# A weight stream of a two-layer trunk on one core: blocks split one by one, or in pairs

## The chip, the cores and the metric

The kernel runs on one core of one Trainium2 chip. The metric is the device time of the program in microseconds (us), one launch, inputs in HBM. TensorE multiplies, VectorE, ScalarE and GpSimd work beside it on tiles of 128 partitions in the on-chip memory, and SyncE issues the loads. The profile calls them PE, DVE, ACT, POOL and SP.

## The reference, cut to what matters

Two layers on 256 tokens of width 1024. Layer 0 mixes by latent attention, layer 1 by attention whose keys an indexer selects; a PEER expert mixer stands behind each. Everything is float32.

```python
for i in range(2):
    m = mla(x) if i == 0 else dsa(x)            # 8 heads; x @ w_in, ..., o @ w_o
    x = layernorm(ALPHA * x + m)
    f = peer(x)
    x = layernorm(ALPHA * x + f)

def peer(x):                                    # 16384 experts = 128 x 128 keys
    q = x @ w_q                                 # 8 heads x 2 halves
    v1, i1 = top_k(q1 @ keys1, 16); v2, i2 = top_k(q2 @ keys2, 16)
    best, pos = top_k(v1[:, None] + v2[None, :], 16)
    gate = softmax(best); expert = i1 * 128 + i2 at pos
    return sum_e gelu(x . w_down[e]) * gate[e] * w_up[e]
```

## The kernel before

**Weights.** All large weights come as 604 blocks of 128 x 1024 floats, in the order of their use, through one `Stream`, `ws`. A block is loaded by SyncE's queue into a tile `raw` (L73), rounded by ScalarE into `hi` (the cast, L85), and `lo = raw - hi` is made by VectorE, in places by GpSimd (the subtraction, L89). Tokens are split likewise into `xh` and `xl`. A product is three matmuls: hi by xh, hi by xl, lo by xh (all matmuls have line L198).

**Buffers and lead.** `raw`, `hi` and `lo` have four buffers of one block each. `get()` hands out block i, has the blocks up to i + 3 split (`AHEAD`) and those up to i + 6 loaded (`DMA_AHEAD`), as buffers come free: a cast into a `hi` tile waits until TensorE has read the block that was there four earlier.

**Stages.** The order in which the program gives work to an engine is kept by each engine; a scheduler moves some of it at build time. The stages of the trace, in order:

- latent attention (to 101 us): input blocks, 7 blocks of `mla_qk`, 2 of values, 8 of the out projection (tiles `y`);
- PEER of layer 0: 16 blocks of queries (tiles `pq`), then 128 blocks of `w_down` (tiles `d`, `proj`, 24 matmuls a block), then 128 of `w_up` (tiles `y`, `rows`, 12 matmuls of 512 columns a block);
- sparse attention of layer 1 (from about 935 us): values 8 blocks, indexer queries 4 and one narrow block of keys (`dsa_ik`), 16 of queries and keys, 8 of the out projection. There `share = 3` gives every third block's subtraction to GpSimd;
- PEER of layer 1, as that of layer 0.

Beside the `d` blocks VectorE and GpSimd pick the experts. `choose()` is a generator of small steps, of which each block takes one or two, from about 165 to 300 us (and 1135 to 1270 us). In its tail each step is a compare of 128 x 800 (L635, VectorE), a multiplication (L637, GpSimd) and a reduction (L640, VectorE). Then `prepare` and `place`, four tokens at a time, make one-hot rows (L681 GpSimd, L682 VectorE, L683 ScalarE) and multiply them on TensorE into tiles `G` (to about 500 us, and again in layer 1). In the `w_up` stage each second block has a cast and a subtraction of 128 x 512 for its tokens (L737, L738).

**Finish.** `finish()` takes the last four blocks of a row product (`STAGGER`) without splitting further ones ahead, does token tile 0 on all four, then tile 1, so that the layer norm of tile 0 (L252 to L261; Square on ScalarE, L255; a power on GpSimd, L258) lies beside the matmuls of tile 1. Then it sets `to_pool = TO_POOL`: the next two subtractions go to GpSimd.

Of the kernel before, what the change touches and what calls it, by code (L numbers as in the profile page):

```python
# [10 lines left out]
F32 = mybir.dt.float32  # L11
F32R = mybir.dt.float32r
# [3 lines left out]
ALU = mybir.AluOpType  # L16
AX = mybir.AxisListType

P = 128
T = 256  # L20
D = 1024
# [19 lines left out]
CELLS = sum(SEG)  # L41
STAGGER = 4
STEPS = (2, 1)
TO_POOL = 2
GSCALE = 2.0 ** 14
TINY = 2.0 ** -40
DSA_POOL = 3
# [1 line left out]


class Stream:
    """Weight blocks [128, w] in order of use, each split into two float32r parts."""

    AHEAD = 3
    DMA_AHEAD = 3

    def __init__(self, tc, nc, raw, hi, lo):
        self.tc, self.hold = tc, None
        self.nc, self.raw, self.hi, self.lo = nc, raw, hi, lo
        self.blocks, self.ready = [], []  # L60
        self.n_loaded = self.n_split = self.n_taken = 0
        self.tiles = []
        self.to_pool = 0
        self.share = 0

    def add(self, src, w=D):
        self.blocks += [(src[i], w) for i in range(src.shape[0])]

    def _load(self, upto):
        while self.n_loaded <= min(upto, len(self.blocks) - 1):  # L70
            src, w = self.blocks[self.n_loaded]
            t = self.raw.tile([P, D], F32, tag="raw", name=f"raw{self.n_loaded}")
            self.last = self.nc.sync.dma_start(t[:, :w], src).ins  # L73
            self.tiles.append(t)
            self.n_loaded += 1

    def _split(self, upto):
        nc = self.nc
        while self.n_split <= min(upto, len(self.blocks) - 1):
            w = self.blocks[self.n_split][1]  # L80
            self._load(self.n_split)
            raw = self.tiles[self.n_split][:, :w]
            hi = self.hi.tile([P, D], F32R, tag="hi", name=f"hi{self.n_split}")[:, :w]
            lo = self.lo.tile([P, D], F32R, tag="lo", name=f"lo{self.n_split}")[:, :w]
            nc.scalar.copy(hi, raw)  # L85
            eng = nc.gpsimd if self.to_pool > 0 or (self.share and self.n_split % self.share == 0) else nc.vector
            self.to_pool -= 1
            with self.tc.issue_after(self.hold) if self.hold is not None else nullcontext():
                eng.tensor_tensor(lo, raw, hi.bitcast(F32), op=ALU.subtract)  # L89
            if eng is nc.vector:  # L90
                self.hold = None
            self.ready.append((hi, lo))
            self.n_split += 1

    def get(self, ahead=None):
        i = self.n_taken
        self.n_taken += 1
        self.fill(i + (self.AHEAD if ahead is None else ahead))
        return self.ready[i]

    def fill(self, upto):
        self._split(upto)
        self._load(upto + self.DMA_AHEAD)


class Arena:
# [27 lines left out]
def tile_trunk(ctx: ExitStack, tc: tile.TileContext, ins, out: bass.AP):  # L134
    nc = tc.nc
    def pool(name, bufs, **kw):
        return ctx.enter_context(tc.tile_pool(name=name, bufs=bufs, **kw))
# [3 lines left out]
    big = pool("big", 1)  # L141
    small = pool("small", 3)
    ohp = pool("ohp", 2)
    raws = pool("raws", 4)
    his = pool("his", 4)
    los = pool("los", 4)
    psp = pool("psp", 4, space=bass.MemoryType.PSUM)
    pyp = pool("pyp", 1, space=bass.MemoryType.PSUM)

# [30 lines left out]
    ws = Stream(tc, nc, raws, his, los)  # L180
# [23 lines left out]
        mm(o, ll, rh, False, stop)  # L204

    def proj(o, blk, w=P):
        """o[w, 256] = block^T x^T over all of D."""
        h, l = blk
        for c in range(NC):
            s = slice(c * w, (c + 1) * w)  # L210
            mm3(o, (h[:, s], l[:, s]), (xh[:, c, :], xl[:, c, :]), c == 0, c == NC - 1)
# [21 lines left out]
        return ins  # L233

    def rows(o4, lhs, blk, start, stop, tiles=(0, 1)):
        """o4[t][nh] += lhs(t)^T block, for a moving block [128, 1024]."""
        h, l = blk
        lh, ll = lhs
        for t in tiles:
            tsl = slice(t * P, (t + 1) * P)  # L240
            todo = [(w, rr, i, n) for i, (w, rr) in enumerate(((lh, h), (lh, l), (ll, h))) for n in range(2)]
            if stop:
                todo.sort(key=lambda z: z[3])
            for w, rr, i, n in todo:
                ins = mm(o4[t][n], w[:, tsl], rr[:, n * 512 : (n + 1) * 512], start and i == 0, stop and i == 2)
        return ins
# [15 lines left out]
        return mean.ins  # L262

    def finish(y4, lhs_of, n, g, b, x, spare, after):
        """The last blocks of a row product, token tile by token tile, each with its layer norm."""
        blks = [ws.get(ahead=0) for _ in range(STAGGER)]
        last = None
        for t in range(2):
            with ExitStack() as order:
                if last is not None:  # L270
                    order.enter_context(tc.issue_after(last.ins))
                for i, blk in enumerate(blks):
                    k = n - STAGGER + i
                    last = rows(y4, lhs_of(k), blk, k == 0, k == n - 1, (t,))
            mean = layernorm(x[t], y4[t], g, b, spare[t], spare[2 + t], spare[4])
        for t in range(2):
            with tc.issue_after(mean):
                done = after(t, spare[t])
        ws.to_pool = TO_POOL
        ws.hold = done.ins if done is not None else None  # L280
# [18 lines left out]
        nc.vector.tensor_tensor(o, t1, xs, op=ALU.add)  # L299

    def attention(qk, v, mask, scale, oh, ol, ar, meanwhile):
        """qk(h) lists (qT, kT) pairs whose products add up; o^T in two parts."""
        sring = ar.ring(6, T)
        tring = ar.ring(2, 384)
        probs = {}
# [57 lines left out]
    def mla():  # L363
        ar = Arena(arena, 0, 30720)
        cos, sin = load_rope(ar, "c_rope64")
        norm = ar.take(5)
# [18 lines left out]
                    nc.gpsimd.tensor_tensor(sq[:, lo, :], sq[:, lo, :], sq[:, i, :], op=ALU.add)  # L385

        def inverse_rms(lo, hi, k):
            """[128 tokens, 2]: one over the root mean square of each token's latent."""
            p = ps(f"ms{k}")
            for t in range(2):  # L390
                mm(p[:, t : t + 1], sq[:, lo, t * P : (t + 1) * P], ones, True, True)
            nc.vector.tensor_scalar(rms[:, k, :], p[:, 0:2], 1.0 / (P * (hi - lo)), RMS_EPS, op0=ALU.mult, op1=ALU.add)
            nc.gpsimd.tensor_tensor(rms[:, k, :], rms[:, k, :], mhalf.to_broadcast([P, 2]), op=ALU.pow)
            return rms[:, k, :]
# [8 lines left out]
        parts = []  # L403
        for i in range(3):
            nc.vector.tensor_scalar(nrm[:, i, :], where[i], norm[:, i : i + 1], None, op0=ALU.mult)
            h, l = [z[i // 2].rearrange("p a b -> p (a b)")[:, (i % 2) * T : (i % 2) * T + T] for z in gq]
# [161 lines left out]
    def peer(li):  # L568
        last = li == DEPTH - 1
# [114 lines left out]
                onehot[g4].append((V, U, L))  # L684

        def place(g4, done):
            """Scatter the gates of four tokens; blocks under `done` already hold gelu."""
            p = py(g4 % 4, f"G{g4}")
            for j, (V, U, L) in enumerate(onehot.pop(g4)):
                mm(p[:, j * P : (j + 1) * P], V, U, True, False)  # L690
# [150 lines left out]
```

## Time and profile before

| what | value |
|---|---|
| time, median of three runs | 1910.81 us (1908.92 to 1911.19) |
| profiled execution, span | 1908.3 us |
| TensorE busy | 97% of the span, granted clock 0.9 or more in 39 of 40 slices |
| VectorE busy | 71%, from five to nine tenths and more by slice |
| ScalarE busy | 55% |
| GpSimd busy | 30%, near full only where one-hot rows are made |
| DMA engines busy | 53% of 16 engines, 332.87 MB |

The span is the time from the first to the last instruction of one profiled execution on the core. No time other than its span is shown for that execution; the three runs lie 0.6 to 2.9 us above it, and the median 2.5 us. Busy shares are means over stages that have different limits.

### The profile page before, as it was taken

The numbers are of one execution on the slowest core, as the hardware profiler recorded it, in microseconds if no ns is written. First come the engines' busy times: TensorE is split into PE (matmuls) and PEld (weight loads), VectorE is DVE, ScalarE is ACT, GpSimd is POOL, SyncE is SP. The second block draws the span as 40 slices with busy tenths as digits, with TensorE's granted clock in tenths as the row PEclk, the third lists the DMA queues.
The fourth block names the chain that finished last, engine by engine and source line by source line (L and its number), as shares of the span: only waits on it lengthen the run. The fifth ranks groups of instructions, "written<-read, shape, count | busy, mean of one in ns | idle before, by whom it ended". The sixth has DMA issues, their size and how long they took to land.

```text
span 1908.3 us, 33460 instructions
## 1 busy us (share of the span) xinstructions
PE 1858.4 (97%) x12562; PEld 1677.8 (88%) x12562; DVE 1359.1 (71%) x2765; ACT 1057.2 (55%) x1833; POOL 580.1 (30%) x654
## 2 busy tenths in 40 slices
PE   8989999999999999999998899999999999999998
PEld 7789999999998888888797799999999988888886
DVE  5569998788766555555669589997888665555555
ACT  6544446777655444444466444458777554444443
POOL 2011336999620000000132103359997400000000
PEclk9999999999999999999999899999999999999999
DMA  6355455444557555555554545554444576555553
GB/s 230 120 201 164 148 177 183 154 154 157 165 175 231 188 189 188 190 190 191 199 165 155 174 148 166 179 185 146 156 155 166 168 228 190 188 189 188 191 189 114
DMA packets 93763, 335.53 MB, mean 176 GB/s; under 512 B 10400, under 2 KB 11424, under 8 KB 93600
## 3 DMA queue, kind: packets, MB, share of 16 engines
q1 hardware_dynamic: 93312, 332.87, 53.0%
q8 instruction: 98, 1.61, 0.3%
q14 instruction: 65, 0.53, 0.1%
q10 hardware_dynamic: 288, 0.52, 0.1%
HBM read 329.16 MB, written 4.19 MB: 175 GB/s over the span
## 4 chain that ended last, share of the span: by engine, by line
PE 63%; issue 25%; DVE 8%; POOL 3%; ACT 1%; DMA 0%; SPq 0%; POOLq 0%; DVEq 0%; ACTq 0%
PE d L198 30%; PE y L198 19%; PE pq L198 5%; PE G L198 3%; POOL VU L681 2%; DVE lo L89 2%; PE q L198 1%; PE v L198 1%; DVE arena L635 1%; DVE arena L640 1%; PE ps L198 1%; DVE arena L261 1%; PE h L198 1%; PE qi L198 1%; PE qn L198 0%
## 5 line engine op out<-in xcount | busy, mean ns | idle before, releaser
L89 DVE TENSOR_TENSOR lo<-raw,hi 128x1024 fp32r<-128x1024 f32 x593 | 752.2, 1271 | 344.6 <-ACT hi L85 343.4
L85 ACT CAST hi<-raw 128x1024 fp32r<-128x1024 f32 x604 | 631.3, 1047 | 607.8 <-PE y L198 225.3
L198 PE MATMUL d<-xh,lo 128*128 128x256 f32 x2048 | 581.0, 284 | 8.1 <-DVE lo L89 8.1
L198 PE MATMUL d<-xh,hi 128*128 128x256 f32 x2048 | 586.0, 286 | 0.0
L198 PE MATMUL d<-xl,hi 128*128 128x256 f32 x2048 | 579.1, 283 | 0.0
L681 POOL TENSOR_SCALAR VU<-iota,i2t 128x128 f16<-128x128 f16 x512 | 424.3, 846 | 83.1 <-PE G L198 58.3
L198 PEld LDWEIGHTS d<-xh,lo 128*128 128x128 f32 x2048 | 386.5, 189 | 10.9 <-DVE lo L89 10.9
L198 PEld LDWEIGHTS d<-xh,hi 128*128 128x128 f32 x2048 | 386.9, 189 | 0.0
L198 PEld LDWEIGHTS d<-xl,hi 128*128 128x128 f32 x2048 | 386.8, 189 | 0.0
L198 PE MATMUL y<-lo,xh 128*128 128x512 f32 x1088 | 345.3, 395 | 0.0
L198 PE MATMUL y<-hi,xh 128*128 128x512 f32 x1088 | 344.6, 395 | 0.0
L198 PE MATMUL y<-hi,xl 128*128 128x512 f32 x1088 | 344.5, 395 | 0.0
L258 POOL TENSOR_TENSOR st<-st,mhalf 128x1 f32<-128x1 f32 x8 | 4.4, 555 | 855.8 <-DVE st L257 855.8
L198 PEld LDWEIGHTS y<-lo,xh 128*128 128x128 f32 x1088 | 204.8, 188 | 48.1 <-DVE lo L89 0.6
L198 PEld LDWEIGHTS y<-hi,xl 128*128 128x128 f32 x1088 | 205.0, 188 | 47.9
L198 PEld LDWEIGHTS y<-hi,xh 128*128 128x128 f32 x1088 | 204.8, 188 | 47.4
L682 DVE TENSOR_SCALAR VU<-iota,i1t,gt 128x128 f16<-128x128 f16 x512 | 140.4, 346 | 72.5 <-PE G L198 56.0
L683 ACT ACTIVATE U<-VU,gr 128x128 f16<-128x128 f16 x512 | 171.1, 397 | 1.0 <-DVE VU L682 0.7
L737 ACT CAST xh<-arena 128x512 fp32r<-128x512 f32 x128 | 79.2, 620 | 153.1 <-PE y L198 147.8
L738 DVE TENSOR_TENSOR xl<-arena,xh 128x512 fp32r<-128x512 f32 x128 | 88.2, 692 | 80.8 <-ACT xh L737 80.8
L637 POOL TENSOR_TENSOR arena<-arena 128x800 f32<-128x800 f32 x32 | 72.5, 2270 | 96.6 <-DVE arena L635 89.2
L198 PE MATMUL G<-VU 128*128 128x128 f16 x512 | 74.0, 222 | 4.3 <-DVE VU L682 2.4
(210 smaller groups left out, 1897.6 us busy)
## 6 DMA issues: line engine op xcount, KB each, us to landing
raw<-in_down SPq DMA_DIRECT2D x256, 512.0 KB, 3.3
raw<-in_up SPq DMA_DIRECT2D x256, 512.0 KB, 4.3
raw<-in_peer_q SPq DMA_DIRECT2D x32, 512.0 KB, 4.2
raw<-in_dsa_qk SPq DMA_DIRECT2D x16, 512.0 KB, 3.2
raw<-in_mla_w_o SPq DMA_DIRECT2D x8, 512.0 KB, 4.1
raw<-in_dsa_v SPq DMA_DIRECT2D x8, 512.0 KB, 4.3
raw<-in_dsa_w_o SPq DMA_DIRECT2D x8, 512.0 KB, 4.2
raw<-in_mla_qk SPq DMA_DIRECT2D x7, 512.0 KB, 5.1
```

What stands on the lines that cost most here:

```text
L85: nc.scalar.copy(hi, raw)
L89: eng.tensor_tensor(lo, raw, hi.bitcast(F32), op=ALU.subtract)
L198: return nc.tensor.matmul(o, l, r, start=start, stop=stop, skip_group_check=True)
L261: nc.vector.scalar_tensor_tensor(r[:, s], z[:, s], st[:, 5:6], b[:, s], op0=ALU.mult, op1=ALU.add)
L635: nc.vector.tensor_tensor(o, iota[:, None, :CELLS].to_broadcast([P, TOPK, CELLS]), posf[t][:, h, :, None].to_broadcast([P, TOPK, CELLS]), ...
L637: nc.gpsimd.tensor_tensor(o, o, cell[t][:, h, None, :].to_broadcast([P, TOPK, CELLS]), op=ALU.mult)
L640: nc.vector.tensor_reduce(exp_[t][:, h - 1, :], held, axis=AX.X, op=ALU.add)
L681: nc.gpsimd.tensor_scalar(V, iota16, i2t[:, t : t + 1], None, op0=ALU.is_equal)
L682: nc.vector.tensor_scalar(U, iota16, i1t[:, t : t + 1], gt[:, t : t + 1], op0=ALU.is_equal, op1=ALU.mult)
L683: nc.scalar.mul(L, U, gr[:, t : t + 1])
L737: nc.scalar.copy(hh, a)
L738: nc.vector.tensor_tensor(al, a, hh.bitcast(F32), op=ALU.subtract)
```

## The change

Consecutive blocks of one weight become a group of two, with tiles of 128 x 2 x 1024: still one load for each block, but one cast and one subtraction for the group. `raw`, `hi` and `lo` have two buffers of a group, in the space of four of a block. `get()` splits the next group when it hands out the first block of one, and loads one group beyond those split. A weight with an odd number of blocks ends in a group of one (`mla_qk` with 7, `dsa_ik` with 1). `finish` takes its four blocks, now two groups, with `ahead=False`. `TO_POOL` counts groups: one group behind each layer norm goes to GpSimd instead of two blocks, and in sparse attention every third group instead of every third block.

```diff
-TO_POOL = 2
+TO_POOL = 1
...
-    AHEAD = 3
-    DMA_AHEAD = 3
...
     def add(self, src, w=D):
-        self.blocks += [(src[i], w) for i in range(src.shape[0])]
+        n = src.shape[0]
+        for i in range(0, n, 2):
+            members = [src[j] for j in range(i, min(i + 2, n))]
+            self.group_of += [(len(self.groups), j == 0) for j in range(len(members))]
+            self.groups.append((members, w))
...
-            t = self.raw.tile([P, D], F32, tag="raw", name=f"raw{self.n_loaded}")
-            self.last = self.nc.sync.dma_start(t[:, :w], src).ins
+            t = self.raw.tile([P, 2, D], F32, tag="raw", name=f"raw{self.n_loaded}")
+            for j, src in enumerate(members):
+                self.last = self.nc.sync.dma_start(t[:, j, :w], src).ins
...
+            hi = self.hi.tile([P, 2, D], F32R, tag="hi", name=f"hi{g}")
+            lo = self.lo.tile([P, 2, D], F32R, tag="lo", name=f"lo{g}")
+            nc.scalar.copy(hi[:, :n, :w], raw[:, :n, :w])
+            eng = nc.gpsimd if self.to_pool > 0 or (self.share and g % self.share == 0) else nc.vector
             self.to_pool -= 1
             with self.tc.issue_after(self.hold) if self.hold is not None else nullcontext():
-                eng.tensor_tensor(lo, raw, hi.bitcast(F32), op=ALU.subtract)
+                eng.tensor_tensor(lo[:, :n, :w], raw[:, :n, :w], hi[:, :n, :w].bitcast(F32), op=ALU.subtract)
...
-    def get(self, ahead=None):
+    def get(self, ahead=True):
         i = self.n_taken
         self.n_taken += 1
-        self.fill(i + (self.AHEAD if ahead is None else ahead))
+        g, first = self.group_of[i]
+        self._split(g + 1 if first and ahead else g)
+        self._load(self.n_split + 1)
         return self.ready[i]
-
-    def fill(self, upto):
-        self._split(upto)
-        self._load(upto + self.DMA_AHEAD)
...
-    raws = pool("raws", 4)
-    his = pool("his", 4)
-    los = pool("los", 4)
+    raws = pool("raws", 2)
+    his = pool("his", 2)
+    los = pool("los", 2)
...
-        blks = [ws.get(ahead=0) for _ in range(STAGGER)]
+        blks = [ws.get(ahead=False) for _ in range(STAGGER)]
```

Lines of the changed kernel stand two higher, that of the subtraction four (L93); the cast is L89 there. The order in which instructions stand on an engine moves at three places. A row is the instruction's number, line, operation, what it writes and reads, and its shape.

First, VectorE in the tail of `choose()` in layer 0. Before:

```order
379 L89 TENSOR_TENSOR lo_2964<-raw_2842,hi_2963 128x1024
380 L635 TENSOR_TENSOR arena<-iota,arena 128x800
381 L640 TENSOR_REDUCE arena<-arena 128x16
382 L89 TENSOR_TENSOR lo_3012<-raw_2879,hi_3011 128x1024
383 L635 TENSOR_TENSOR arena<-iota,arena 128x800
384 L640 TENSOR_REDUCE arena<-arena 128x16
385 L89 TENSOR_TENSOR lo_3054<-raw_2927,hi_3053 128x1024
386 L635 TENSOR_TENSOR arena<-iota,arena 128x800
387 L640 TENSOR_REDUCE arena<-arena 128x16
```

After, the same place:

```order
364 L93 TENSOR_TENSOR lo_2618<-raw_2477,hi_2617 128x2048
365 L653 TENSOR_TENSOR arena<-arena,gs 128x128
366 L642 TENSOR_REDUCE arena<-arena 128x16 x2
367 L637 TENSOR_TENSOR arena<-iota,arena 128x800 x2
368 L93 TENSOR_TENSOR lo_2690<-raw_2549,hi_2689 128x2048
369 L642 TENSOR_REDUCE arena<-arena 128x16 x2
370 L637 TENSOR_TENSOR arena<-iota,arena 128x800 x2
371 L93 TENSOR_TENSOR lo_2773<-raw_2621,hi_2772 128x2048
372 L642 TENSOR_REDUCE arena<-arena 128x16 x2
373 L637 TENSOR_TENSOR arena<-iota,arena 128x800
374 L93 TENSOR_TENSOR lo_2858<-raw_2693,hi_2857 128x2048
```

A subtraction of one block stood behind each compare and reduction; now one of two blocks stands behind two reductions and one or two compares.

Second, ScalarE at the end of the `w_up` stage of layer 0: casts (`hi`), the tokens' casts (`xh`), and the Square of the layer norm. Before:

```order
714 L85 CAST hi_9948<-raw_9894 128x1024
715 L85 CAST hi_9966<-raw_9914 128x1024
716 L85 CAST hi_9986<-raw_9932 128x1024
717 L85 CAST hi_10004<-raw_9952 128x1024
718 L85 CAST hi_10022<-raw_9970 128x1024
719 L255 ACTIVATE arena,st<-arena,st 128x1024
720 L85 CAST hi_10137<-raw_9990 128x1024
721 L85 CAST hi_10141<-raw_10008 128x1024
722 L85 CAST hi_10145<-raw_10026 128x1024
```

After:

```order
552 L89 CAST hi_9189<-raw_9127 128x2048
553 L739 CAST xh<-arena 128x512
554 L89 CAST hi_9222<-raw_9160 128x2048
555 L89 CAST hi_9255<-raw_9193 128x2048
556 L89 CAST hi_9286<-raw_9226 128x2048
557 L257 ACTIVATE arena,st<-arena,st 128x1024
558 L89 CAST hi_9402<-raw_9259 128x2048
559 L89 CAST hi_9406<-raw_9290 128x2048
```

Ahead of the Square stand five casts of one block, of which the last four are those of `finish`; now four of two blocks, of which the last two are those of `finish`. The next casts stand behind the Square as before.

Third, GpSimd in sparse attention: L298 (L300 after) is a multiplication of the rotary embedding. Before:

```order
42 L298 TENSOR_TENSOR arena<-arena 128x512 x2
43 L89 TENSOR_TENSOR lo_10509<-raw_10406,hi_10508 128x1024
44 L298 TENSOR_TENSOR arena<-arena 128x512
45 L89 TENSOR_TENSOR lo_10664<-raw_10512,hi_10663 128x1024
46 L298 TENSOR_TENSOR arena<-arena 128x512 x2
47 L89 TENSOR_TENSOR lo_10809<-raw_10667,hi_10808 128x1024
48 L298 TENSOR_TENSOR arena<-arena 128x512
49 L89 TENSOR_TENSOR lo_10911<-raw_10812,hi_10910 128x1024
50 L298 TENSOR_TENSOR arena<-arena 128x512 x2
51 L89 TENSOR_TENSOR lo_11007<-raw_10914,hi_11006 128x1024
```

After:

```order
38 L300 TENSOR_TENSOR arena<-arena 128x512 x2
39 L93 TENSOR_TENSOR lo_9703<-raw_9604,hi_9702 128x2048
40 L300 TENSOR_TENSOR arena<-arena 128x512 x2
41 L93 TENSOR_TENSOR lo_9988<-raw_9771,hi_9987 128x2048
42 L300 TENSOR_TENSOR arena<-arena 128x512 x3
43 L93 TENSOR_TENSOR lo_10171<-raw_10052,hi_10170 128x2048
44 L300 TENSOR_TENSOR arena<-arena 128x512 x3
45 L260 TENSOR_TENSOR st<-st,mhalf 128x1
```

Five subtractions of one block become three of two blocks.

## Rows read from the trace of the kernel before

**Rows 1.** The page: span, busy us of each engine (share), instructions.
```profile
span 1908.3 us, 33460 instructions
...
PE 1858.4 (97%) x12562; PEld 1677.8 (88%) x12562; DVE 1359.1 (71%) x2765; ACT 1057.2 (55%) x1833; POOL 580.1 (30%) x654
```

**Rows 2.** The chain that ended last (start us, us, what).
```profile
354.11 5.75 PE d L198 x48
...
1543.66 350.91 PE y L198 x1510
```

**Rows 3.** Groups on ScalarE by shape, 600 to 900 us (busy us, mean ns).
```profile
L85 ACT CAST hi<-raw 128x1024 fp32r<-128x1024 f32 x108 | 113.2, 1048 | 90.8 <-PE y L198 90.8
L737 ACT CAST xh<-arena 128x512 fp32r<-128x512 f32 x54 | 33.5, 620 | 68.8 <-PE y L198 68.8
```

**Rows 4.** Groups on VectorE by shape, 600 to 900 us.
```profile
L89 DVE TENSOR_TENSOR lo<-raw,hi 128x1024 fp32r<-128x1024 f32 x108 | 132.3, 1225 | 95.1 <-ACT hi L85 95.0
L738 DVE TENSOR_TENSOR xl<-arena,xh 128x512 fp32r<-128x512 f32 x54 | 37.4, 693 | 36.4 <-ACT xh L737 36.4
```

**Rows 5.** Timeline of ScalarE around 921 us (start us, us, what, idle before).
```profile
921.02 1.05 ACT L85 CAST hi<-raw 128x1024 fp32r<-128x1024 f32 x1 [1.74 <-PE y L198]
```

**Rows 6.** The weight tiles raw, 1012.9 to 1013.9 us: issues and their landing.
```profile
L73 SPq DMA_DIRECT2D raw<-in_dsa_w_o x2: 328/356/383, 1013.1 to 1013.5; - x2
...
DMA to landing us min/median/max: 3.3/3.7/4.1
```

**Rows 7.** The same view, 700 to 730 us.
```profile
DMA to landing us min/median/max: 4.2/4.3/4.5
```

**Rows 8.** Busy us of each engine in a stretch (first number: its length).
```profile
260.00:280.00 20.00, 19.29 (x162) 19.09 (x161) 19.97 (x32) 10.70 (x13) 9.19 (x5) 1.00 0.46 153
```

**Rows 9.** The page's costliest groups: the one-hot compare on GpSimd.
```profile
L681 POOL TENSOR_SCALAR VU<-iota,i2t 128x128 f16<-128x128 f16 x512 | 424.3, 846 | 83.1 <-PE G L198 58.3
```

**Rows 10.** Groups on VectorE by shape, 185 to 300 us.
```profile
L89 DVE TENSOR_TENSOR lo<-raw,hi 128x1024 fp32r<-128x1024 f32 x39 | 60.6, 1560 | 0.1
```

**Rows 11.** Timeline of VectorE, 276.3 to 280.2 us.
```profile
276.33 2.10 DVE L89 TENSOR_TENSOR lo<-raw,hi 128x1024 fp32r<-128x1024 f32 x1
278.35 0.98 DVE L635 TENSOR_TENSOR arena<-iota,arena 128x800 f32<-128x800 f32 x1
279.25 0.97 DVE L640 TENSOR_REDUCE arena<-arena 128x16 f32<-128x800 f32 x1
```

**Rows 12.** Timeline of GpSimd in the same stretch.
```profile
275.59 1.75 POOL L637 TENSOR_TENSOR arena<-arena 128x800 f32<-128x800 f32 x1 [2.06 <-DVE arena L635]
```

**Rows 13.** Waits of TensorE, 185 to 300 us (us in total, times, longest).
```profile
PE d L198 <- DVE lo L89: 4.0, 6, 0.7
```

**Rows 14.** Timeline of ScalarE, the out projection of layer 0.
```profile
88.64 3.89 ACT L85 CAST hi<-raw 128x1024 fp32r<-128x1024 f32 x4 [5.91 <-PE y L198]
```

**Rows 15.** Timeline of VectorE, the layer norm behind it.
```profile
97.55 1.29 DVE L256 SCALAR_TENSOR_TENSOR arena<-arena,st 128x1024 f32<-128x1024 f32 x1
...
99.64 3.55 DVE L261 SCALAR_TENSOR_TENSOR arena<-arena,st 128x512 f32<-128x512 f32 x2 [0.66 <-POOL st L258]
...
104.69 1.81 DVE L256 SCALAR_TENSOR_TENSOR arena<-arena,st 128x1024 f32<-128x1024 f32 x1
```

**Rows 16.** Timeline of GpSimd in the same stretch.
```profile
99.81 5.60 POOL L89 TENSOR_TENSOR lo<-raw,hi 128x1024 fp32r<-128x1024 f32 x2 [0.21 <-ACT hi L85]
```

**Rows 17.** Timeline of ScalarE at the start.
```profile
4.14 1.04 ACT L85 CAST hi<-raw 128x1024 fp32r<-128x1024 f32 x1 [2.14 <-DMA raw<-in_mla_h]
```

**Rows 18.** Groups on GpSimd, sparse attention, 960 to 1025 us.
```profile
L89 POOL TENSOR_TENSOR lo<-raw,hi 128x1024 fp32r<-128x1024 f32 x5 | 13.0, 2609 | 7.8 <-ACT hi L85 5.8 <-DVE arena L522 2.0
```

**Rows 19.** Timeline of VectorE, sparse attention.
```profile
999.25 2.59 DVE L541 SCALAR_TENSOR_TENSOR arena<-arena 128x256 f32<-128x256 f32 x1
...
1002.03 0.47 DVE L541 SCALAR_TENSOR_TENSOR arena<-arena 128x256 f32<-128x256 f32 x1
```

**Rows 20.** Timeline of GpSimd in the same stretch.
```profile
998.96 2.60 POOL L89 TENSOR_TENSOR lo<-raw,hi 128x1024 fp32r<-128x1024 f32 x1 [0.71 <-ACT hi L85]
```

More of the change, by code (lines that the diff above doesn't have):

```diff
@@ L59, in __init__ @@
         self.nc, self.raw, self.hi, self.lo = nc, raw, hi, lo
-        self.blocks, self.ready = [], []
+        self.groups, self.group_of, self.ready = [], [], []
         self.n_loaded = self.n_split = self.n_taken = 0
@@ L66, in add @@
     def add(self, src, w=D):
-        self.blocks += [(src[i], w) for i in range(src.shape[0])]
-    def _load(self, upto):
-        while self.n_loaded <= min(upto, len(self.blocks) - 1):
-            src, w = self.blocks[self.n_loaded]
-            t = self.raw.tile([P, D], F32, tag="raw", name=f"raw{self.n_loaded}")
-            self.last = self.nc.sync.dma_start(t[:, :w], src).ins
+        n = src.shape[0]
[3 more added lines that the diff above has]
+            self.groups.append((members, w))
+    def _load(self, upto):
+        while self.n_loaded <= min(upto, len(self.groups) - 1):
+            members, w = self.groups[self.n_loaded]
+            t = self.raw.tile([P, 2, D], F32, tag="raw", name=f"raw{self.n_loaded}")
+            for j, src in enumerate(members):
+                self.last = self.nc.sync.dma_start(t[:, j, :w], src).ins
             self.tiles.append(t)
@@ L78, in _split @@
         nc = self.nc
[L79 to L86, printed above, removed]
+        while self.n_split <= min(upto, len(self.groups) - 1):
+            g = self.n_split
+            members, w = self.groups[g]
+            n = len(members)
+            self._load(g)
+            raw = self.tiles[g]
+            hi = self.hi.tile([P, 2, D], F32R, tag="hi", name=f"hi{g}")
+            lo = self.lo.tile([P, 2, D], F32R, tag="lo", name=f"lo{g}")
+            nc.scalar.copy(hi[:, :n, :w], raw[:, :n, :w])
+            eng = nc.gpsimd if self.to_pool > 0 or (self.share and g % self.share == 0) else nc.vector
             self.to_pool -= 1
             with self.tc.issue_after(self.hold) if self.hold is not None else nullcontext():
-                eng.tensor_tensor(lo, raw, hi.bitcast(F32), op=ALU.subtract)
+                eng.tensor_tensor(lo[:, :n, :w], raw[:, :n, :w], hi[:, :n, :w].bitcast(F32), op=ALU.subtract)
             if eng is nc.vector:
                 self.hold = None
-            self.ready.append((hi, lo))
+            self.ready += [(hi[:, j, :w], lo[:, j, :w]) for j in range(n)]
             self.n_split += 1
-    def get(self, ahead=None):
+    def get(self, ahead=True):
         i = self.n_taken
         self.n_taken += 1
-        self.fill(i + (self.AHEAD if ahead is None else ahead))
+        g, first = self.group_of[i]
+        self._split(g + 1 if first and ahead else g)
+        self._load(self.n_split + 1)
         return self.ready[i]
-    def fill(self, upto):
-        self._split(upto)
-        self._load(upto + self.DMA_AHEAD)
 class Arena:
```

## The prediction

> **What bounds the kernel now.** I read the page first, then the chain, then each stage's groups. The page shows TensorE busy for 97% of the span [rows 1], so a cheaper split can return only the few per cent in which TensorE waits; what an edit costs is read from the places where a split becomes ready late. The chain gives TensorE's pace: 48 matmuls of a `d` stage, two blocks, in 5.75 us, and 1510 of the last `y` stage in 350.91 us without a gap, 0.232 us each, so 2.79 us for a block of 12 and 5.58 us for two [rows 2].
>
> Splitting one block costs ScalarE 1.048 us and VectorE 1.225 us where nothing disturbs them [rows 3, 4]; the subtraction's idle time there is ended by the cast, so it runs right behind it. The cast starts when TensorE lets go of a buffer: at 921.02, after 1.74 us idle for `y` [rows 5]. I take 0.2 us from the last matmul's end to the cast's start, an estimate.
>
> **Price of a pair.** The 512-wide casts and subtractions give the slope: 1.048 - 0.620 = 0.428 us and 1.225 - 0.693 = 0.532 us for 512 more columns [rows 3, 4]. A pair of 2048 columns then costs 1.048 + 2 x 0.428 = 1.90 us on ScalarE and 1.225 + 2 x 0.532 = 2.29 us on VectorE. Two single ones cost 2.10 and 2.45. So each pair saves 0.2 us of ScalarE and 0.16 us of VectorE, about 57 and 48 us over 300 pairs, on engines that are not the bound of the whole.
>
> The change also moves the lead. Before, the split of block i + 3 is asked for when block i starts, into the buffer just freed; its `lo` is ready 0.2 + 1.05 + 1.2 = 2.45 us later and needed 3 blocks later, after 8.6 us: lead 6.2 us. After, the split of a pair starts when the pair before the current one is done and takes 0.2 + 1.9 + 2.3 = 4.4 us; its `lo` is needed one pair later: 5.75 - 4.4 = 1.35 us of lead in the `d` stages. Where a stage is smooth, 1.35 us is as good as 6.2; where VectorE is late by more, TensorE now stands.
>
> **Where it stays hidden, costed at nothing.** In the `y` stages a pair needs 4.4 us of 5.58, plus 0.46 us for the two matmuls that only need `hi`: slack about 1.6 us, some of which the token casts and subtractions (0.62 and 0.69 us a pair) take. Loads: an isolated pair, issued at 1013.1 and 1013.5, lands 3.3 and 4.1 us after its issues, so the second 4.5 us after the first issue [rows 6]; in the `y` stage a landing takes 4.3 us [rows 7], so a pair takes about 4.3 + 1.4 = 5.7 us (an estimate that keeps the 1.2 us between the two landings of rows 6). A `raw` buffer is free as soon as its subtraction is done, and the next cast comes one pair (5.58) plus the rest of its chain later, about 6.8 us: hidden by 1 us. In the stretches with `place`, GpSimd sets the pace with 8 compares of 0.846 us for two blocks, 6.8 us [rows 9]; that gives a pair 1 us more slack than a bare `d` stage. Were this cover gone, each 0.1 us would cost 0.1 us on each of about 250 pairs, 25 us. The queries' stage has slack too.
>
> **Choosing experts, the largest term.** From about 165 to 300 us, and again in layer 1, VectorE is full: 19.97 of 20 us from 260 on [rows 8]. Its 39 single subtractions there take 1.560 us in the mean instead of 1.225 [rows 10]. The timeline tells why: the one at 276.33 takes 2.10 us while GpSimd's L637 runs from 275.59 to 277.34, that is, it starts to move when GpSimd is done [rows 11, 12]. The Trainium skill, "SBUF — State Buffer", section "SBUF: two separate sides", says that the port pair which the two share is an exclusive lock that one instruction holds to its end; this trace agrees, 2.10 beside 1.225 us. In the tail one block takes VectorE 2.02 + 0.90 + 0.90 = 3.82 us [rows 11] against 2.87 us of TensorE; the lead of 6.2 us absorbs nearly all, and TensorE waits 4.0 us, in 6 waits of at most 0.7 us [rows 13].
>
> After, by the order shown, a pair in the tail takes VectorE a subtraction of 2.2 us (back to back), two reductions of 0.9 and two compares of 0.9, and 0.75 to 1.65 us each for the port or for GpSimd's product: about 8.15 us, against 5.75 us of TensorE, and two such pairs follow each other: 4.8 us late, with 1.35 us of lead. I went through the 23 pairs of this stage in the changed order with these prices. TensorE waits ten times, 0.1 to 3.55 us, together 11.1 us; 9.4 us if the subtraction always gets the port first. Less the 4.0 us of before that is 5.4 to 7.1 us; as the view of waits leaves out the shortest gaps of before, I take the lower end, 5.5 us, twice: **+11 us** (0 to 16; the 0 is the rival below).
>
> **Finish.** The last pair's cast needs the buffer of the third last, free only when `finish` begins. Token tile 0 of one pair takes 2.79 us plus 0.46, the last pair's `lo` 4.4 us: 1.15 us of waiting, in both PEERs **+2.4**. In the out projections four blocks are used up side by side; before, the four next casts began while that still ran [rows 14] and were ready in time. After, the first pair is released 1.4 us before the end and its `lo` comes 3.0 us after it, 0.46 us being covered: 2.5 us, twice **+5.0**. Bounds for both: 2 and 10 us.
>
> **Layer norms.** Two GpSimd subtractions, 5.60 us together, hold the port in the first one's place: L261 takes 3.55 us for two, and L256 1.81 instead of 1.29 [rows 15, 16]. One pair on GpSimd takes about 4.8 us in one piece, so the instruction that meets it waits for its whole rest instead of slipping in between the two: 0.8 us at three places, **+2.4** (0 to 6).
>
> **Start.** The first cast starts at 4.14 us when its load has landed [rows 17]. A pair's second load lands 1.2 us later, the cast is 0.85 us longer, the subtraction 1.1 us, and `xl` stands behind it: 3.1 us, of which later waits for input loads take back some: **+2.4** (1 to 4).
>
> **Groups of one.** `mla_qk`'s seventh block gives the pair behind it 2.87 us for a chain of 4.4: 4.4 - 2.87 = **+1.5** (0 to 3). Behind `dsa_ik` the same less what the first matmuls cover, 1.3. In sparse attention GpSimd's subtractions take 2.609 us [rows 18]; a pair takes about 4.8, so its `lo` comes 0.2 + 1.9 + 4.8 = 6.9 us after the release, against 5.75: late by 0.9, three times. And it holds the port twice as long: an L541 that takes 0.47 us alone took 2.59 behind the subtraction at 998.96 [rows 19, 20]; after, the selection on VectorE stands up to 2.2 us longer, and the next pair's subtraction behind it. Together about **+5.4** (2 to 9).
>
> **Sum.** 2.4 + 1.5 + 5.0 + 2.4 + 2.4 + 11 + 5.4 = 30.1 us on a span of 1908.3: 1938.4. The median run lies 2.5 us above the span, so 1941 us.
>
> **Rivals.** *Faster.* In the choosing stage VectorE is the bound, and half as many subtractions meet the port half as often: (1.560 - 1.225) x 39 = 13 us of stretch per layer, half of it gone, and 0.16 us for each pair besides. If VectorE's backlog shrinks by that much, TensorE's 4.0 us there go in both layers, 8 us, and the other terms must stay under this: 1902 to 1905 us. It decides if the late pairs are late by less than the 1.35 us lead. The Trainium skill, "Perfetto Trace Analysis", section "Optimizing Scalar/DVE Operations", says that larger operations help an engine that is saturated, and that where an engine is not saturated but makes others wait, smaller ones let work complete sooner. Here VectorE is saturated by the first half and makes TensorE wait by the second, so the page alone does not decide. Against the rival: VectorE's tail work per pair (8.15 us) stays above 5.75 in any case, and the late part is then one pair at once. Chance 0.08.
>
> *No change.* The waits fall where TensorE already waits for something else (the gaps at the layer norms) and the saving in VectorE pays the rest: 1908 to 1914. Chance 0.06.
>
> *Worse.* The steady stages lose their slack: a pair's loads land later than the 6.8 us, or the chain is longer than 4.4 us by more than 1.6. At 0.1 to 0.3 us on 250 pairs this adds 25 to 75 us: 1966 to 2016. For it speaks that the DMA estimate has a margin of only 1 us; against it, that the 4.3 us already hold the queueing of neighbouring loads, and pairs ask for no more bytes. Chance 0.14.
>
> *The forecast*, slower by waits at the seven places and not in the steady stages: 0.72, with its own range 1921 to 1955 from the bounds (lower ends 1 + 0 + 2 + 0 + 2 with half the choosing term, 10.5 us; the upper ends sum to 48 us, but hardly meet).
>
> **Numbers.** A measurement tells no change from changes under 0.2%, 3.8 us. Faster 0.08, same 0.06, slower 0.72 + 0.14 = 0.86. The range leaves out the faster and the same case and the upper part of the worse one: 1920 to 1970.
>
> **What would show it.** Right: subtractions of 2.2 to 2.4 us where undisturbed and casts of 1.9; TensorE's waits for `lo` in the choosing stretch near 10 us per layer, with single waits over 2 us in the tail; a wait of about 1 us at the end of each `w_up` stage and 2.5 in each out projection; no waits in the `y` stages, which keep 0.232 us a matmul. Wrong: waits for loads or casts repeated each pair in the `y` stages (the worse rival); a choosing stretch that takes no longer than before (the faster one); a pair's cast or subtraction that is much dearer than its slope says.

## The result and the profile after

The changed kernel takes 1938.4 us (median of four runs, 1935.1 to 1941.0), against 1910.4 us before: ratio 1.014, interval 1.0128 to 1.0153, so 28 us slower. The profiled execution is the shortest of the four: span 1933.4 us, 25.1 us above that of before [rows 1].

First the page: the span, the engines, and the groups of the pairs' subtraction and cast.

```profile
span 1933.4 us, 32274 instructions
...
PE 1863.0 (96%) x12562; PEld 1681.4 (87%) x12562; DVE 1319.0 (68%) x2469; ACT 1005.0 (52%) x1532; POOL 639.3 (33%) x649
...
L93 DVE TENSOR_TENSOR lo<-raw,hi 128x2048 fp32r<-128x2048 f32 x297 | 689.1, 2321 | 254.5 <-ACT hi L89 254.4
L89 ACT CAST hi<-raw 128x2048 fp32r<-128x2048 f32 x303 | 575.1, 1899 | 429.6 <-PE d L200 280.4
```

ScalarE and VectorE do less: the casts 575 us, the subtractions 689 us. TensorE is busy nearly as long as before (1863 against 1858 us; the lower clock told below makes matmuls longer); the rest of the 25 us are waits. TensorE's largest waits for a split, for the first operands and for a layer norm (us in total, times, longest; `xt` are transposes, which TensorE makes too, `h` is the first product):

```profile
PE d L200 <- DVE lo L93: 15.7, 13, 3.0
PE xt L230 <- DVE arena L263: 13.5, 2, 6.8
PE h L200 <- ACT xh L765: 9.4, 1, 9.4
PE y L200 <- DVE lo L93: 5.3, 4, 1.6
PE h L200 <- DVE xl L767: 2.9, 1, 2.9
PE q L200 <- DVE lo L93: 2.7, 2, 1.6
...
PE y L200 <- ACT hi L89: 1.2, 2, 0.6
```

The same view of the kernel before, the three largest:

```profile
PE xt L228 <- DVE arena L261: 13.3, 5, 5.3
PE d L198 <- DVE lo L89: 8.1, 12, 0.7
PE h L198 <- ACT xh L763: 5.8, 1, 5.8
```

Waits alone do not say where the end moved, since some are paid back. So I set the two traces beside each other: both have 12562 matmuls, and the offset is the start of the k-th in one less that in the other. The table gives the offset that each stage adds (difference of the median offset over some tens of matmuls at its end and at the one before; us). Inside some stages the order of the matmuls differs between the two traces, so the offsets are read at the ends. "Again" is a second execution of the changed kernel, the last two columns are experiments told below.

| stage (its end before) | forecast | changed | again | single instructions | three buffers |
|---|---|---|---|---|---|
| latent attention, to its out projection (85 us) | 3.9 | 3.4 | 3.5 | -0.7 | 0.7 |
| out projection, layer norm, queries (171 us) | 3.3 | 2.7 | 2.3 | -0.3 | 0.7 |
| choosing and one-hot stretch, layer 0 (384 us) | 5.5 | 4.5 | 4.5 | 4.7 | 7.8 |
| to the end of `w_up` (899 us) | 0 | 0.1 | 0.4 | 1.1 | -0.1 |
| finish, layer norm, values (961 us) | 2.0 | 3.3 | 4.5 | -1.4 | 0.6 |
| sparse attention (1048 us) | 5.4 | 2.6 | 4.1 | 1.7 | 3.1 |
| out projection, layer norm, queries (1138 us) | 3.3 | 2.9 | 3.0 | -1.3 | 0.1 |
| choosing and one-hot stretch, layer 1 (1355 us) | 5.5 | 3.7 | 3.4 | 5.2 | 7.8 |
| `w_up` and the last finish (1908 us) | 1.2 | 1.8 | 1.7 | 0.9 | -0.2 |
| sum | 30.1 | 25.0 | 27.4 | 9.9 | 20.5 |

The tail of the choosing, VectorE's timeline (compare [rows 11]):

```profile
274.25 3.83 DVE L93 TENSOR_TENSOR lo<-raw,hi 128x2048 fp32r<-128x2048 f32 x1
278.00 0.97 DVE L642 TENSOR_REDUCE arena<-arena 128x16 f32<-128x800 f32 x1
279.73 0.99 DVE L642 TENSOR_REDUCE arena<-arena 128x16 f32<-128x800 f32 x1 [0.76 <-POOL arena L639]
280.63 1.88 DVE L637 TENSOR_TENSOR arena<-iota,arena 128x800 f32<-128x800 f32 x2
282.43 3.86 DVE L93 TENSOR_TENSOR lo<-raw,hi 128x2048 fp32r<-128x2048 f32 x1
```

and GpSimd's, two products in one row (compare [rows 12]):

```profile
273.50 6.19 POOL L639 TENSOR_TENSOR arena<-arena 128x800 f32<-128x800 f32 x2 [2.92 <-DVE arena L637]
```

A pair takes VectorE 282.43 - 274.25 = 8.18 us. The subtraction takes 3.83 instead of 2.29 us, since it waits behind the first product; the second product then starts behind the subtraction, and the second reduction waits 0.76 us for it.

What I had not in the sum is the clock. Windows of the changed kernel (length; busy of TensorE, its weight loads, VectorE, ScalarE, GpSimd; granted clock, DMA share, GB/s):

```profile
280.00:284.00 4.00, 4.00 (x35) 3.89 (x33) 4.00 (x4) 0.22 (x1) 2.31 (x1) 1.00 0.48 188
284.00:288.00 4.00, 1.75 (x12) 1.66 (x12) 3.25 (x3) 2.18 (x2) 3.90 (x2) 0.89 0.18 47
288.00:292.00 4.00, 4.00 (x26) 4.00 (x26) 4.00 (x4) 0.00 (x0) 2.10 (x1) 0.68 0.54 215
...
1000.00:1004.00 4.00, 4.00 (x36) 4.00 (x35) 4.00 (x5) 1.60 (x6) 2.31 (x1) 1.00 0.38 116
```

and of its second execution:

```profile
1000.00:1004.00 4.00, 4.00 (x22) 4.00 (x22) 2.94 (x3) 2.87 (x7) 1.82 (x1) 0.58 0.45 179
```

Between 284 and 288 us TensorE stands for 4.00 - 1.75 = 2.25 us, waiting for a `lo`; then its clock falls to the lower level, 1.2 GHz, for a while: over 284 to 292 us (0.11 + 0.32) x 4 = 1.7 us of full clock are missing, and 26 matmuls run in the last 4 us where 35 did in the first. In the kernel before the clock never falls in the `d` stages.

### The profile page after: what moved, and what is told of

Same layout as the page of the kernel before. It is cut to its first block, busy times and chain, and to the rows that moved or that the text cites. A ratio compares the mean times of both kernels' runs of the same rounds, so it can differ in the third digit from the quotient of the medians.

```text
span 1933.4 us, 32274 instructions
## 1 busy us (share of the span) xinstructions
PE 1863.0 (96%) x12562; PEld 1681.4 (87%) x12562; DVE 1319.0 (68%) x2469; ACT 1005.0 (52%) x1532; POOL 639.3 (33%) x649
## 4 chain that ended last, share of the span: by engine, by line
PE 71%; DVE 13%; POOL 9%; issue 5%; ACT 1%; DMA 0%; DVEq 0%; SPq 0%; POOLq 0%; ACTq 0%
PE y L200 38%; PE d L200 20%; POOL VU L683 7%; PE pq L200 5%; DVE lo L93 5%; PE G L200 2%; POOL arena L639 2%; DVE arena L637 1%; PE h L200 1%; PE s L200 1%; DVE arena L609 1%; DVE arena L607 1%; DVE arena L642 1%; PE ps L200 1%; ACT hi L89 1%
## 5 line engine op out<-in xcount | busy, mean ns | idle before, releaser
L93 DVE TENSOR_TENSOR lo<-raw,hi 128x2048 fp32r<-128x2048 f32 x297 | 689.1, 2321 | 254.5 <-ACT hi L89 254.4
L89 ACT CAST hi<-raw 128x2048 fp32r<-128x2048 f32 x303 | 575.1, 1899 | 429.6 <-PE d L200 280.4
L200 PE MATMUL d<-xh,lo 128*128 128x256 f32 x2048 | 581.8, 284 | 15.8 <-DVE lo L93 15.7
L683 POOL TENSOR_SCALAR VU<-iota,i2t 128x128 f16<-128x128 f16 x512 | 457.0, 910 | 72.0 <-PE G L200 32.9
L200 PE MATMUL y<-hi,xh 128*128 128x512 f32 x1088 | 325.3, 395 | 1.2 <-ACT hi L89 1.2
L639 POOL TENSOR_TENSOR arena<-arena 128x800 f32<-128x800 f32 x32 | 94.7, 2970 | 67.4 <-DVE arena L637 67.4
L624 POOL TENSOR_TENSOR arena<-arena 128x8 f32<-128x8 f32 (+4 forms) x64 | 21.8, 382 | 180.1 <-DVE arena L619 180.1
```

The costliest lines, as they stand in the source:

```text
L89: nc.scalar.copy(hi[:, :n, :w], raw[:, :n, :w])
L93: eng.tensor_tensor(lo[:, :n, :w], raw[:, :n, :w], hi[:, :n, :w].bitcast(F32), op=ALU.subtract)
L200: return nc.tensor.matmul(o, l, r, start=start, stop=stop, skip_group_check=True)
L624: nc.gpsimd.tensor_tensor(cell[t][:, :, w], ih[:, :, 1, 0 : SEG[a]], ih[:, :, 0, a : a + 1].to_broadcast([P, HEADS, SEG[a]]), op=ALU.add)
L639: nc.gpsimd.tensor_tensor(o, o, cell[t][:, h, None, :].to_broadcast([P, TOPK, CELLS]), op=ALU.mult)
L683: nc.gpsimd.tensor_scalar(V, iota16, i2t[:, t : t + 1], None, op0=ALU.is_equal)
```

## The experiments

The changes are to the changed kernel unless the text says "before".

**One instruction for each block, in pair tiles** (`single_ops`).

```diff
-            nc.scalar.copy(hi[:, :n, :w], raw[:, :n, :w])
+            for j in range(n):
+                nc.scalar.copy(hi[:, j, :w], raw[:, j, :w])
...
-                eng.tensor_tensor(lo[:, :n, :w], ...)
+                for j in range(n):
+                    eng.tensor_tensor(lo[:, j, :w], ...)
```

> Pair tiles and two buffers of a pair as in the changed kernel, but one cast and one subtraction for each block. If the time was lost because a pair is one piece, of which nothing is ready until 4.4 us after its release (the lead), the first block's lo comes 0.2 + 1.05 + 1.2 = 2.45 us after it, and most of the loss goes: 1912 to 1922 us, with waits of TensorE for lo in the choosing stretch back near 4 us and none at the end of the w_up stages. If it was lost because buffers come free only two blocks at a time (rival), the time stays at 1930 to 1940 us.

1920.1 us, ratio to before 1.0044 (1.0030 to 1.0058): two thirds of the loss go. Start, out projections, finish and layer norms lose nothing more. Of the waits in the `w_up` and out projection stages this is left:

```profile
PE y L202 <- DVE lo L95: 1.1, 2, 0.5
```

But the two choosing stretches still lose 4.7 and 5.2 us, and TensorE's waits for `lo` there stay at 8.4 us to 300 us, not 4: half of the expectation missed. So in the choosing the long instruction alone is not what costs; what these tiles still share with the pairs are two buffers, given free two blocks at a time, and a shorter lead than before.

**Only the subtraction, or only the cast, for each block** (`single_subs`, `single_casts`: one half of the diff above).

> The changed kernel with one cast for a pair, but one subtraction for each block. Lead: the first lo comes 0.2 + 1.9 + 1.2 = 3.3 us after the release instead of 4.4, the wait at the end of the w_up stages falls from 1.2 us to about 0.1, that of the out projections to 1.5, and GpSimd holds the port half as long at a time: 1917 to 1928 us. Release in pairs: 1930 to 1940 us.

> The changed kernel with one cast for each block, but one subtraction for a pair. Lead: lo of both blocks still comes 0.2 + 2.1 + 2.3 = 4.6 us after the release, so nothing is won: 1935 to 1942 us. If the longer cast on ScalarE were what costs (rival), the time falls below 1930 us.

1932.6 us (ratio 1.0112, 1.0095 to 1.0129) and 1939.5 us (1.0148, 1.0131 to 1.0165). Single casts win nothing, as expected, since `lo` waits for both. Single subtractions win only about 6 us; that misses the expectation and lies in the range that it gave to the rival. The pair's cast, which still holds back the first block, would be a reason; no run shows that it is the whole one, and the choosing of layer 0 loses 5.9 us here. Neither half gives what both give.

**Less lead with single blocks** (`hi2`, `hi3`; of the kernel before, the first shown).

```diff
-    AHEAD = 3
+    AHEAD = 1
...
-    his = pool("his", 4)
-    los = pool("los", 4)
+    his = pool("his", 2)
+    los = pool("los", 2)
...
-STAGGER = 4
+STAGGER = 2
```

> The kernel before with single blocks throughout, but two instead of four buffers of hi and lo, one block split ahead, and two blocks instead of four in finish; raw keeps four buffers. The split of a block then starts when the block before the current one is done: a lead of 2.87 + 0.24 - 2.45 = 0.66 us in the d stages, less than the 1.35 us of the pairs, with small instructions. If the lead is what costs in the choosing stretch, it takes at least 5 us longer there in each layer and the whole 1920 to 1935 us; if the size of the instructions is what costs (rival), the stretch is as before, and the whole within 4 us of 1910.

> The kernel before with three instead of four buffers of hi and lo for single blocks, two blocks split ahead, and three blocks in finish. The lead in the d stages is 2 x 2.87 + 0.24 - 2.45 = 3.5 us, near that of single instructions in pair tiles (3.3 us), which lost 4.8 us in the choosing stretch and what follows to 500 us. If the lead decides there, this kernel loses 2 to 5 us in that stretch of each layer and takes 1914 to 1922 us; if the release of buffers two at a time did it (rival), it loses under 1 us there.

1971.6 us (ratio 1.0319, 1.0302 to 1.0336) and 1933.8 us (1.0121, 1.0105 to 1.0138). With two buffers the choosing stretches lose 17.1 and 17.0 us, with three 7.8 each; most of the rest of `hi2` lies at the layer norms, and may go with its shorter finish, which I did not separate. Waits of the three-buffer kernel, 170 to 305 us:

```profile
PE d L198 <- DVE lo L89: 9.2, 9, 2.5
```

No pair and no long instruction is in these kernels, so fewer buffers and a shorter lead alone are enough to lose time in the choosing. Both kernels lose more than I expected and miss their ranges. The lead as I computed it does not put the kernels in order: 3.5 us lose 7.8 us here, 3.3 us lose 4.7 and 5.2 with single instructions in pair tiles, and the 1.35 us of the pairs lose 4.5 and 3.7. That pairs give VectorE less work is a reason for the last (see the next runs); what sets the first two apart stays open, and pairs with more buffers were not run.

**The port in the choosing's tail** (`after_no_product`, `before_no_product`).

```diff
-                        nc.gpsimd.tensor_tensor(o, o, cell[t][:, h, None, :].to_broadcast([P, TOPK, CELLS]), op=ALU.mult)
+                        nc.gpsimd.tensor_tensor(o[:, :, 0:1], o[:, :, 0:1], cell[t][:, h, None, 0:1].to_broadcast([P, TOPK, 1]), op=ALU.mult)
```

> The changed kernel with GpSimd's product of 128 x 800 in the tail of the choosing cut to 128 x 16 (the experts are then not the chosen ones), so that GpSimd hardly holds the port beside the subtractions. A pair in the tail then takes VectorE 2.2 + 1.8 + 1.8 = 5.8 us against 5.75 of TensorE. If the late subtractions there come from the port, TensorE's waits for lo from 170 to 300 us fall from 7.9 to under 2 us, and the granted clock does not fall in that stretch. If the pairs' lead alone makes them (rival), 5 us or more of waits are left.

> The kernel before with the same product cut to 128 x 16. A block in the tail then takes VectorE 1.1 + 0.9 + 0.9 = 2.9 us against 2.87 of TensorE: the waits for lo there fall from 4.0 us to under 1, and the time by 5 to 10 us, to 1901 to 1906. The changed kernel without the product should be 13 to 19 us slower than this one, instead of 28: what is left is start, out projections, finish, layer norms and sparse attention.

1914.1 and 1900.8 us, one run each: 13.3 us apart instead of 28. Waits of the changed kernel without the product, 170 to 300 us:

```profile
PE d L200 <- DVE lo L93: 0.6, 2, 0.4
```

Nor does the granted clock fall in that stretch any more. Against the full kernel before, the stretch to 384 us now takes the pairs 7.2 us less and the single blocks 5.1 us less. Without the product the pairs are the faster ones there, by 2.1 and 1.6 us in the two layers. So the rival's saving in VectorE's work is real, and the `lo` that comes late beside the product is what turns it round. The edit takes two things out at once, the product's hold on the port and VectorE's wait for its result (the 0.76 us above); for pairs no run parts the two.

**The first blocks alone** (`start_singles`).

```diff
-    ws.add(ins["mla_h"][0:6])
+    ws.add(ins["mla_h"][0:1])
+    ws.add(ins["mla_h"][1:2])
+    ws.add(ins["mla_h"][2:6])
```

> The changed kernel with the first two blocks as groups of one; everything else in pairs. The first matmul of the changed kernel starts 3.7 us later than before and its stage is 4.8 us late, of which 3.4 are left at the end of the latent attention. If that is the first pair's load, cast and subtraction in one piece, the offset to the kernel before falls to 0 to 1.5 us there, and the whole is 2 to 4 us shorter than the changed kernel: 1933 to 1937 us. If the loads of the input set the pace (rival), 3 us or more are left at that place and the time stays near 1938.

1934.8 us (ratio 1.0120, 1.0103 to 1.0137); the offset at 85 us is 0.4 us instead of 3.4. In the whole this is not clear: the intervals overlap, and in the trace 1.4 us go again in the out projection, where the granted clock falls (92 to 100 us: 0.79). Part of the 3.4 us is not the pair's size. ScalarE's start in the kernel before, then in the changed one:

```profile
0.72 1.28 ACT L85 ACT_TABLE_LOAD   x1 [0.72 <-PEq L831]
...
5.68 1.28 ACT L89 ACT_TABLE_LOAD   x1 [5.68 <-DMA raw<-in_mla_h]
6.98 1.90 ACT L89 CAST hi<-raw 128x2048 fp32r<-128x2048 f32 x1
```

The cast of a pair waits for two loads, and the table load ahead of it, which ran at 0.72 us before, now stands behind one of these waits, which ends at 5.68 us: 1.28 us on the path [rows 17]. With the first block alone it runs at 0.72 us again.

**GpSimd's share** (`no_share`: `ws.share = 0`; `pool_halves`: on GpSimd one subtraction for each block).

> The changed kernel with no subtraction on GpSimd in sparse attention (the share of every third pair goes to VectorE); behind the layer norms GpSimd still takes one pair. If GpSimd's long subtractions, which hold the port, cost the 2.6 us there, the offset to the kernel before grows by 0 to 1 us over that stage, and the whole is 1 to 3 us shorter than 1938. If VectorE has no room beside the selection (rival), the stage grows by more than 3 us.

> The changed kernel, with each pair that goes to GpSimd subtracted as two instructions of one block. If one long hold of the port costs 0.8 us at each of three layer norms and delays the selection in sparse attention, the whole is 2 to 5 us shorter than the changed kernel, 1933 to 1936 us. If the place of the long hold is covered (rival), it stays at 1938, and the offset to the kernel before grows as much across the layer norms as in the changed kernel.

1936.8 us (ratio 1.0138, 1.0121 to 1.0155) and 1931.5 us (1.0105, 1.0088 to 1.0122). Without the share sparse attention adds 2.6 us as before, and the intervals overlap: no gain is clear. But the waits are others, 958 to 1060 us:

```profile
PE s L200 <- DVE m L319: 2.8, 2, 2.0
...
PE q L200 <- DVE lo L93: 1.2, 1, 1.2
```

Of the two late `lo` (2.7 us) one is left (1.2 us). In place of the other there are 2.8 us of waits for the softmax, and the granted clock falls at 1052 to 1056 us, 0.57 against 1.00 in the first trace of the changed kernel. The timelines tell what the other late `lo` hung on. GpSimd, VectorE and ScalarE in the changed kernel (L543 is a step of the selection):

```profile
1012.69 4.57 POOL L93 TENSOR_TENSOR lo<-raw,hi 128x2048 fp32r<-128x2048 f32 x1 [3.10 <-ACT hi L89]
...
1014.65 2.90 DVE L543 SCALAR_TENSOR_TENSOR arena<-arena 128x256 f32<-128x256 f32 x1
...
1020.58 1.90 ACT L89 CAST hi<-raw 128x2048 fp32r<-128x2048 f32 x1
...
1025.40 2.27 DVE L93 TENSOR_TENSOR lo<-raw,hi 128x2048 fp32r<-128x2048 f32 x1
```

VectorE at the same place without the share:

```profile
1015.16 0.71 DVE L543 SCALAR_TENSOR_TENSOR arena<-arena 128x256 f32<-128x256 f32 x1
...
1022.77 2.29 DVE L93 TENSOR_TENSOR lo<-raw,hi 128x2048 fp32r<-128x2048 f32 x1 [1.37 <-ACT hi L89]
```

Beside GpSimd's long subtraction the selection's step takes 2.90 us instead of 0.71, and VectorE comes to the next subtraction 2.9 us after its cast has ended; without the share it starts as soon as the cast is done. Halves on GpSimd take the same wait away:

```profile
PE q L201 <- DVE lo L94: 1.2, 1, 1.2
```

Halves on GpSimd are 7 us faster by the medians, more than expected. The transposes' wait behind the layer norms falls from 13.5 us to

```profile
PE xt L231 <- DVE arena L264: 10.9, 2, 5.4
```

and the stage with the finish and values adds 0.5 us instead of 3.3, with no lower clock behind it. The trace, of the slowest of the four runs, has a span only 0.4 us shorter than that of the changed kernel, and lower clock elsewhere (1052 to 1056 us: 0.72), so it does not show where the rest of the 7 us lies.

**A second trace** (`after_again`, no edit).

> The changed kernel once more, for a second trace of the same program. If the spread of its runs (1935 to 1941 us) comes from TensorE's granted clock falling after some of its waits in one execution and not in another, this trace differs from the first by the number of such stretches, each of about 3.4 us at half clock and 1.5 us of loss, with the same waits. If it comes from the loads (rival), the waits for loads differ and the clock does not.

1937.5 us, span 1935.7. Its waits are those of the first (15.8 and 15.7 us for `lo` in the `d` stages), but the clock also falls at 1000 to 1004 us, 0.58 against 1.00 in the windows above, and for twice as long at 948 to 956. These two stages hold the whole difference (4.5 and 4.1 us in place of 3.3 and 2.6).

**A faster kernel before** (`before_half_products`).

```diff
-                        nc.gpsimd.tensor_tensor(o, o, cell[t][:, h, None, :].to_broadcast([P, TOPK, CELLS]), op=ALU.mult)
+                        for z in (slice(0, 8), slice(8, 16)):
+                            nc.gpsimd.tensor_tensor(o[:, z, :], o[:, z, :], cell[t][:, h, None, :].to_broadcast([P, 8, CELLS]), op=ALU.mult)
```

> The kernel before, with GpSimd's product of 128 x 800 in the tail of the choosing made as two of 128 x 400; nothing else is changed. If a subtraction waits only for the instruction that holds the port, it waits about 0.1 us instead of 1.0 beside the first half, a block in the tail takes VectorE about 3.0 us instead of 3.82, TensorE's waits for lo there fall from 4.0 us to under 2, and the time falls by 3 to 8 us, to 1903 to 1908: faster than both kernels. If GpSimd takes the port again at once for the second half (rival), the time stays at 1910 to 1912.

1905.5 us, ratio 0.9974 (0.9964 to 0.9983): 5 us faster than before, and faster than both kernels. VectorE's tail, then GpSimd's, then TensorE's waits from 170 to 300 us:

```profile
274.11 1.38 DVE L89 TENSOR_TENSOR lo<-raw,hi 128x1024 fp32r<-128x1024 f32 x1
275.40 1.77 DVE L635 TENSOR_TENSOR arena<-iota,arena 128x800 f32<-128x800 f32 x1
277.09 0.97 DVE L641 TENSOR_REDUCE arena<-arena 128x16 f32<-128x800 f32 x1
277.99 1.38 DVE L89 TENSOR_TENSOR lo<-raw,hi 128x1024 fp32r<-128x1024 f32 x1
```

```profile
273.43 2.89 POOL L638 TENSOR_TENSOR arena<-arena 128x400 f32<-128x400 f32 x2 [0.99 <-DVE arena L635]
```

```profile
PE d L198 <- DVE lo L89: 2.1, 3, 0.8
```

The subtraction now takes 1.38 instead of 2.10 us, so `lo` comes 0.7 us sooner. But the tail is no shorter, 277.99 - 274.11 = 3.88 us: the compare now waits for the second half (1.77 instead of 0.98 us). The wait was moved behind the instruction that TensorE waits for, not removed; that part of my expectation was wrong. The Trainium skill, "SBUF — State Buffer", section "SBUF: two separate sides", has the loser stand until the holding instruction ends. The halves agree: the subtraction waits for the first half alone (0.97 us of the 2.89).

## Why the prediction was right

It gave 1941 us; the median is 1938.4. On the traced spans it gave 30.1 us more, and 25.1 were measured. The direction, the places and the prices hold. Several terms have the wrong size, the clock was left out, and the errors partly cancel: that the total comes so near is in part luck.

- **Price of a pair:** right. Cast 1.90 us (1.899 in the mean), subtraction 2.28 to 2.29 undisturbed, as worked out from the slope.
- **What stays hidden:** right. The `w_up` stages add nothing up to their finish, and have no wait for loads or casts; the worse rival is out. (The sum for the loads there adds 1.4 us where its words say 1.2; nothing hung on it.)
- **Finish:** right. 1.1 us at the end of the `w_up` stage of layer 0 against 1.15. In the out projections 0.6 + 1.6 = 2.2 us, against 2.5; the chain shows the two links one behind the other:

```profile
92.76 1.91 ACT hi L89
...
94.70 2.30 DVE lo L93
...
97.04 3.06 PE y L200 x12
```

- **Layer norms:** right mechanism, wrong size. GpSimd's one instruction holds up the next tile's L258 (L256 before, [rows 15, 16]):

```profile
107.29 4.54 POOL L93 TENSOR_TENSOR lo<-raw,hi 128x2048 fp32r<-128x2048 f32 x1 [1.79 <-ACT hi L89]
```

```profile
109.02 3.89 DVE L258 SCALAR_TENSOR_TENSOR arena<-arena,st 128x1024 f32<-128x1024 f32 x1
```

3.89 us instead of 1.81. TensorE's waits for the transposes there, before and after:

```profile
PE xt L228 <- DVE arena L261: 6.2, 2, 5.3
```

```profile
PE xt L230 <- DVE arena L263: 6.8, 1, 6.8
```

The longest wait grows by 1.5 us, but a shorter one goes, so the sum grows by 0.6; the offset grows by 0.3 and 0.5 us at the two layer norms behind out projections, not by 0.8 each. At the third, behind the `w_up` stage of layer 0, it grows by 2.0 us. There the waits sum to 3.5 us as before, and the granted clock falls (948 to 952 us: 0.67).
- **Start and groups of one:** 3.4 us for both against 3.9, but made up otherwise: 4.8 us at the start (forecast 2.4, without the table load), 1.4 taken back later, and no wait behind `mla_qk` (forecast 1.5). That the two sums agree is luck.
- **Choosing:** right in the work (8.18 us a pair against 8.15) and in the cause (the product on GpSimd, shown by taking it out, and the lead, as far as the runs with fewer buffers show it), too large in the sum: 4.5 and 3.7 us instead of 5.5 each. TensorE's waits to 310 us are 7.9 us, not 9.4 to 11.1. At the peak, near 275 us of the kernel before, the offset had grown by 9.5 us, and 5.0 came back by 384 us: there the kernel before still pays for a late VectorE and GpSimd (its waits behind 277 us), and the changed one does not. My step took TensorE's waits as lost, and looked only to 300 us.
- **Sparse attention:** 2.6 us in place of 5.4. The term that failed is a `lo` of GpSimd that comes 0.9 us late, three times: TensorE waits for none of these here. The other two parts hold. The pair behind `dsa_ik` is the first late `lo`, 1.2 us (forecast 1.3); its cast starts when TensorE is done with the queries (`qi`) ahead of that narrow block:

```profile
985.74 1.91 ACT L89 CAST hi<-raw 128x2048 fp32r<-128x2048 f32 x1 [2.64 <-PE qi L200]
...
987.69 2.29 DVE L93 TENSOR_TENSOR lo<-raw,hi 128x2048 fp32r<-128x2048 f32 x1 [2.50 <-ACT hi L89]
```

The second, 1.6 us, is the subtraction behind a selection that GpSimd's long subtraction holds up, as the prediction has it; both kernels that shorten or drop that subtraction lose this wait. That dropping it shows no gain in the whole is the exchange told above; why the softmax then waits longer stays open.
- **Left out of the sum:** the clock. In the first trace it falls four times where it did not before (in 220 to 228, 284 to 292, 948 to 956 and 1256 to 1264 us), each time 1.7 us of full clock missing. By an estimate from the 284 us stretch, where some 16 matmuls start 0.213 us apart instead of 0.119, that is 1.5 us each, so up to 6 of the 25 us, inside the stages' figures above; TensorE's busy time grew by 4.6 us in all.

Of the rivals, the faster one had the right saving and the wrong sign: VectorE's work shrinks, and without GpSimd's product that shows.

## What to carry to other kernels

Two blocks in one instruction save work, which pays only on an engine that bounds the kernel; they also make every result of the pair as late as the last one, and take away lead. Count the lead (time until the result is needed less the chain that makes it) for each stage, above all where the preparing engine is full or shares a port, and at the ends of stages. A computed lead tells where to look; here it did not put the kernels in order. Where an engine must hold a port that another one waits for, shorter instructions on the first one may pay: GpSimd's product in two halves gave 5 us.

## What the runs showed of the hardware that I had not expected

- After waits of TensorE of 1.9, 2.25 and 3.0 us inside a stage of matmuls (they end at 221, 286 and 1260 us) the granted clock fell from 2.4 to 1.2 GHz and rose again with the matmuls going on; after one of 3.0 us that ends at 278 us it did not (280 to 284 us: 1.00). The same program took such falls in one execution and not in another, with the same waits (1000 to 1004 us: 1.00 and 0.58). The two profiled spans of the changed kernel, 1933.4 and 1935.7 us, differ by about this.
- The activation table's load moved behind a wait for a load when the first cast came to wait for two: it ran at 5.68 us instead of 0.72, and at 0.72 again when the first cast waited for one load.
- One GpSimd subtraction of 2048 columns took 4.54 us where two of 1024 took 5.60 together [rows 16], and yet the transposes' waits grew, 6.8 us in place of 6.2.
